# Three column blocks of the first modulation moved from TensorE to VectorE at the start of a two-layer diffusion backbone

## Chip, cores and metric

The kernel runs on one core of a Trainium2 chip. The metric is the device time of one execution in microseconds (us); lower is better. TensorE is written PE in the rows of the profile, VectorE DVE, ScalarE ACT, GpSimd POOL, and SP is the engine that issues most of the transfers.

## The reference, cut to what matters

Each of two layers modulates its input with a shift and a scale that come from the conditioning, projects it, mixes tokens in four branches, and goes on to an MLP. Only the very beginning of layer 0 bears on the change:

```
def _layer(x, cond, lp, mixer_fn):
    mod = jax.nn.silu(cond) @ lp['w_ada'] + lp['b_ada']
    sh1, sc1, g1, sh2, sc2, g2 = jnp.split(mod[:, None, :], 6, axis=-1)
    y, extra = mixer_fn(x * (1 + sc1) + sh1)
    ...
def _project(h, lp):
    ...
    (q_lat, kv_lat, k_pe, ...) = jnp.split(h @ lp['w_in'], split_at, axis=-1)
```

There are 384 tokens (128 with the conditioning `c_ctx`, 256 with `c`), D_MODEL is 1024, and everything is float32. The transposed input `h` is 8 blocks of 128 channels. Each block needs 128 shifts and 128 scales for two conditionings: one *unit* of `mod`, a product of silu(cond) with a 1024 x 256 piece of `w_ada`.

## The kernel before

A product in near float32 precision is made of three matmuls: an operand is split into a high part (fp32r) and a low remainder, `x = xh + xl`, and xh·wh, xh·wl and xl·wh are added up in PSUM. ScalarE makes the high part of a weight tile (a CAST, line 281), VectorE the low one (`split_low`, line 125).

The start of layer 0 (lines 470 to 557) interleaves three things for k = 0 to 7:

- `first_part(k)`: the modulation product of unit k on TensorE (line 330: eight small f32 matmuls of 32 x 256, sixteen records), whose bank ScalarE copies to `adap` (line 333).
- `first_input(k)`: `ada_finish` turns `adap` round with two TensorE transposes (line 339); VectorE sums the four row groups (341), adds the bias into `modT` (343) and 1 to the scale (492). Then ScalarE writes the high part of the modulated input, `hTh` (496, two instructions), VectorE the full value `hx` (497) and the low part `hTl` (125).
- `chunk(banks, w, n, k)`: nine matmuls of block k with the weights of branch A (`banks_a`, 416 columns, tiles named `o`) or of branch C (`banks_c`, 512 columns, tiles `wh` and `wl`). First the high parts (lines 520, 521), then the three that read `hTl` (518). `within` is called after the second of the three token blocks, so `ada_finish` of a coming unit stands inside a chunk.

I call the A chunk of block k a(k) and the C chunk c(k). `split_w(i)` splits the weights for blocks 2i and 2i+1. The loop runs over pairs: a(k), product k+1, c(k), the split, product k+2, a(k+1), c(k+1); the last two chunks are c(7), a(7). TensorE's order is pinned to the program by `in_order`; the other engines' instructions are placed by the scheduler. The DMA queue of SP loads everything in the order of use: two 512 KB pieces of `w_ada` per unit, the input block, and two weight tiles per pair.

After the map ScalarE evacuates the banks (`evac_to`, line 594, tiles `tmc`, `tma`); the next projection (lines 120 to 122) needs one of the C banks back. `cond_rows` (lines 226 to 233) makes `csr`, the silu of both conditionings on all 128 partitions, from a broadcast load of 1 MB: four tanh on ScalarE and eight instructions on VectorE, behind the map. `csr` feeds `ada_vector` (line 370), which computes later modulation columns on VectorE as sums of products along rows: one custom instruction of 128 x 1024 for each 128 columns and conditioning.

## Time and profile before

| | |
|---|---|
| median of 3 runs | 1311.73 us (1308.55 to 1313.06) |
| profiled execution, its own time | 1311.86 us |
| span of its instructions | 1310.1 us, so 1.8 us lie around it |
| mean granted TensorE clock | 0.993 |
| start of the first chunk, a(0) | 10.30 us |
| start of the first matmul behind the map | 56.25 us |

The profiled execution lies 0.13 us above the median. TensorE is the engine that is busy for nearly all of the span. [...]

### The profile page before, as it was taken

What the parts mean: (1) busy time and instruction counts of PE and PEld (TensorE: products, weight loads), DVE (VectorE), ACT (ScalarE), POOL (GpSimd) and SP (SyncE); (2) the same over time, 40 slices, a digit from 0 to 9 for tenths busy, and PEclk for the clock granted to TensorE, in tenths of its full rate; (3) what the DMA queues carried; (4) which work ended last, traced back from release to release, by engine and by line L of the source; (5) the groups of instructions that cost most, each with busy time, mean ns of one, the idle gap of its engine ahead of it and who ended that gap; (6) DMA issues with size and microseconds to landing.
All of it is one profiled execution on the core that took longest, in us unless ns stands there. A gap on an engine that the chain in (4) does not pass through costs nothing. (4 is left out here: it accounts for less than half of the span.)

```text
span 1310.1 us, 19402 instructions
## 1 busy us (share of the span) xinstructions
PE 1273.6 (97%) x7350; PEld 1143.7 (87%) x7350; DVE 882.9 (67%) x1603; ACT 572.7 (44%) x1054; POOL 207.2 (16%) x218
## 2 busy tenths in 40 slices
PE   8899999999999999999999999999999899999996
PEld 5789888999987999999988988899998799999995
DVE  4555899996669999543484689967455893333336
ACT  4454345323534444454365545423343644444441
POOL 0010301323223000000071120012320600000003
PEclk9999999999999999999999999999999999999998
DMA  9832354666534888554313224553644263335321
GB/s 368 295 109 91 103 173 158 210 217 222 163 112 163 274 272 271 177 171 140 113 72 121 86 93 161 182 173 118 227 159 153 72 225 129 129 129 183 133 71 49
DMA packets 64686, 211.68 MB, mean 162 GB/s; under 512 B 9233, under 2 KB 13265, under 8 KB 64465
## 3 DMA queue, kind: packets, MB, share of 16 engines
q1 hardware_dynamic: 61872, 201.49, 45.6%
q0 software_dynamic: 2432, 8.42, 1.9%
q8 instruction: 58, 0.95, 0.3%
q10 hardware_dynamic: 288, 0.52, 0.1%
q14 instruction: 36, 0.29, 0.1%
HBM read 206.28 MB, written 4.13 MB: 161 GB/s over the span
## 5 line engine op out<-in xcount | busy, mean ns | idle before, releaser
L125 DVE TENSOR_TENSOR wl<-raw,wh 128x1024 fp32r<-128x1024 f32 x250 | 317.5, 1274 | 284.9 <-ACT wh L281 281.2
L281 ACT CAST wh<-raw 128x1024 fp32r<-128x1024 f32 x250 | 261.7, 1050 | 453.3 <-PE bank L121 300.0
L120 PE MATMUL bank<-hTh,wh 128*128 128x384 f32 x976 | 330.8, 339 | 0.0
L122 PE MATMUL bank<-hTh,wl 128*128 128x384 f32 x976 | 328.1, 336 | 0.0
L121 PE MATMUL bank<-hTl,wh 128*128 128x384 f32 x976 | 328.0, 336 | 0.0
L120 PEld LDWEIGHTS bank<-hTh,wh 128*128 128x128 f32 x976 | 183.8, 188 | 6.7 <-issue 2.2
L121 PEld LDWEIGHTS bank<-hTl,wh 128*128 128x128 f32 x976 | 183.7, 188 | 2.4 <-issue 0.3
L122 PEld LDWEIGHTS bank<-hTh,wl 128*128 128x128 f32 x976 | 183.7, 188 | 0.6 <-issue 0.3
L121 PE MATMUL bank<-wl,uh 128*128 128x512 f32 x384 | 150.4, 392 | 0.0
L122 PE MATMUL bank<-wh,ul 128*128 128x512 f32 x384 | 150.2, 392 | 0.0
L120 PE MATMUL bank<-wh,uh 128*128 128x512 f32 x384 | 149.4, 391 | 0.0
L370 DVE CUSTOM_DVE_ANT_0 acc<-raw,csr,bT 128x1024 bf16<-128x1024 f32 x80 | 103.7, 1319 | 0.0
L120 PE MATMUL bank<-wh,hTh 128*128 128x256 f32 x336 | 100.6, 299 | 2.8 <-ACT tmc L594 2.8
L1107 POOL TENSOR_TENSOR tt<-tt,tt 128x384 f32<-128x384 f32 x48 | 61.6, 1304 | 242.3 <-DVE tt L1106 235.7
L370 DVE CUSTOM_DVE_ANT_0 acc<-lnc,csr,bT 128x1024 bf16<-128x1024 f32 x80 | 99.6, 1278 | 0.0
L121 PE MATMUL bank<-wl,hTh 128*128 128x256 f32 x336 | 96.0, 286 | 0.0
L122 PE MATMUL bank<-wh,hTl 128*128 128x256 f32 x336 | 95.9, 285 | 0.0
L120 PEld LDWEIGHTS bank<-wh,uh 128*128 128x128 f32 x384 | 72.0, 188 | 15.4 <-ACT wh L281 0.8
L122 PEld LDWEIGHTS bank<-wh,ul 128*128 128x128 f32 x384 | 72.0, 188 | 15.0
L121 PEld LDWEIGHTS bank<-wl,uh 128*128 128x128 f32 x384 | 72.1, 188 | 13.8
L120 PEld LDWEIGHTS bank<-wh,hTh 128*128 128x128 f32 x336 | 64.7, 193 | 6.8 <-ACT tmc L594 3.1
L121 PEld LDWEIGHTS bank<-wl,hTh 128*128 128x128 f32 x336 | 64.8, 193 | 2.5 <-issue 1.6
(260 smaller groups left out, 1862.3 us busy)
## 6 DMA issues: line engine op xcount, KB each, us to landing
raw<-in_w_g_dram SPq DMA_DIRECT2D x64, 512.0 KB, 3.6
raw<-in_w_d_dram SPq DMA_DIRECT2D x64, 512.0 KB, 3.5
raw<-in_w_u_dram SPq DMA_DIRECT2D x58, 512.0 KB, 3.7
raw<-in_w_av_dram SPq DMA_DIRECT2D x40, 512.0 KB, 3.4
lnc<-in_w_av_dram SPq DMA_DIRECT2D x40, 512.0 KB, 4.4
raw<-in_w_q_dram SPq DMA_DIRECT2D x28, 512.0 KB, 4.5
raw<-in_w_ada_dram SPq DMA_DIRECT2D x16, 512.0 KB, 8.5
raw<-in_w_b_dram SPq DMA_DIRECT2D x16, 512.0 KB, 3.6
```

Source lines behind the costliest of these rows:

```text
L120: mm(out, lhsT=a_hl[0], rhs=b_hl[0], start=start, stop=False)
L121: mm(out, lhsT=a_hl[0], rhs=b_hl[1], start=False, stop=False)
L122: mm(out, lhsT=a_hl[1], rhs=b_hl[0], start=False, stop=stop)
L125: nc.vector.tensor_tensor(out=low, in0=x, in1=high.bitcast(F32), op=ALU.subtract)
L281: nc.scalar.copy(wh, raw)
L370: nc.vector.tensor_tensor_reduce(out=alloc().bitcast(BF16), in0=w, in1=csr[:, c], scale=1.0, scalar=bT[:, l, u, b:b + 1], op0=ALU.mult, op ...
L1107: nc.gpsimd.tensor_tensor(out=acc[c], in0=acc[c], in1=t_, op=ALU.add)
```

## The change

Units 3, 5 and 7 are no longer multiplied on TensorE. Their pieces of `w_ada` are stored transposed (`w_as`), and VectorE sums them along rows against `csr` (`row_sums`, four custom instructions for each unit), bias included, straight into `modT`. For that `csr` must exist early: `cond_rows` now loads 8 KB into one partition, TensorE spreads it over 128 partitions by four f32 matmuls with a row of halves, and ScalarE and VectorE make x·(1 + tanh x) of the banks. In the units that stay on TensorE, a product with a 0/1 matrix `sel` takes the place of the transposes and of VectorE's sum. The 1 for the scale is added to the bias once. Except for unit 0, `hx` is now written by ScalarE. The first weights are loaded in two pieces and split in four; three more warm-up matmuls stand ahead of a(0). The first two stream tiles are split by name ahead of c(7), as the scheduler did before. `in_order()` now pins ScalarE and VectorE to the program's order as well.

```
-    def cond_rows(alloc):
-        nc.sync.dma_start(out=csr, in_=a["cond"].partition_broadcast(P))
...
+    def cond_rows(banks, alloc):
+        crow, half = alloc([1, 2 * D], "crow", 1), alloc([1, P], "half", 1)
+        nc.scalar.dma_start(out=crow, in_=a["cond"].rearrange("(o c) d -> o (c d)", o=1))
+        nc.vector.memset(half, 0.5)
...
+            mm(b, lhsT=half, rhs=crow[:, i:i + 512], start=True, stop=True)
+        for c, h, b in parts:
+            th = alloc([P, 512], "th", 2)
+            nc.scalar.activation(th, b, AF.Tanh)
+            nc.vector.scalar_tensor_tensor(out=csr[:, c, h * 512:(h + 1) * 512], in0=th, scalar=1.0, in1=b, op0=ALU.add,
+                                           op1=ALU.mult)
...
         for b in range(2):
-            nc.tensor.transpose(pt[:, b * P:(b + 1) * P], part[:, b * P:(b + 1) * P], ident)
-        red = sb.tile([P, 2, 2], F32, tag="adar", name=nm("adar"), bufs=2)
...
+            mm(pt[:, 2 * b:2 * b + 2], lhsT=part[:, b * P:(b + 1) * P], rhs=sel, start=True, stop=True)
...
+                def row_sums(k, c):
+                    if k in ROW_UNITS:
+                        for b in range(2):
+                            junk = st.tile([P, 512], F32, tag="junk", name=nm("junk"), bufs=1)
+                            nc.vector.tensor_tensor_reduce(
+                                out=junk.bitcast(BF16), in0=inputs[k][0][b], in1=csr[:, c], scale=1.0,
+                                scalar=bT[:, 0, k, b:b + 1], op0=ALU.mult, op1=ALU.add,
+                                accum_out=modT[0][:, k, b, c:c + 1])
...
+                        else:
+                            nc.scalar.activation(hx[:, cs], xk[:, cs], AF.Identity, bias=sh, scale=m)
                     split_low(hT[1][:, k, :], hx, hT[0][:, k, :])
...
-                with in_order((mybir.EngineType.PE,)):
+                with in_order():
...
                     for k in range(0, KT, 2):
...
                             split_w(k // 2 + 1)
                             first_part(k + 2)
                             chunk(banks_a, w_a, A_W, k + 1, lambda: first_input(k + 2))
+                            for c in range(2):
+                                row_sums(k + 3, c)
                             chunk(banks_c, w_c, 512, k + 1)
                         else:
+                            for i in range(SPLITS_AHEAD):
+                                stream.split(i)
```

**ScalarE, from the input of block 1 to that of block 3.** `adap` is the copy of a unit's product, `o` and `wh` are the weights' high parts, `hTh` and `hx` the modulated input. Before:

```order
L333 COPY adap_299<-bank_290 128x256
L281 CAST o_282<-raw_141 128x832
L496 ACTIVATE hTh<-xk_139,modT_102,ms_114 128x256
L496 ACTIVATE hTh<-xk_139,modT_102,ms_114 128x128
L281 CAST wh_286<-raw_143 128x1024
L333 COPY adap_350<-bank_341 128x256
```

Now (`adap_325` and `xk_140` belong to unit 2, `xk_150` to unit 3):

```order
L529 ACTIVATE hx_297<-xk_134,modT_102 128x128
L529 ACTIVATE hx_297<-xk_134,modT_102 128x256
L289 CAST o_308<-raw_142 128x832
L289 CAST wh_312<-raw_144 128x1024
L340 COPY adap_325<-bank_316 128x256
L521 ACTIVATE hTh<-xk_140,modT_102 128x128
L521 ACTIVATE hTh<-xk_140,modT_102 128x256
L529 ACTIVATE hx_335<-xk_140,modT_102 128x128
L529 ACTIVATE hx_335<-xk_140,modT_102 128x256
L521 ACTIVATE hTh<-xk_150,modT_102 128x128
L521 ACTIVATE hTh<-xk_150,modT_102 128x256
```

The copy of a unit's product stood ahead of the two CASTs and now stands behind both; two `hx` follow each pair of `hTh`.

**VectorE, the same stretch.** `wl` and the second `o` are the low parts of the weights; an ISA row with `junk` is one row sum. Before:

```order
L343 TENSOR_TENSOR modT_102<-adar_308,bT 128x4
L492 TENSOR_SCALAR ms_114<-modT_102 128x2
L497 TENSOR_SCALAR hx_312<-xk_139,ms_114,modT_102 128x256
L497 TENSOR_SCALAR hx_312<-xk_139,ms_114,modT_102 128x128
L125 TENSOR_TENSOR o_283<-raw_141,o_282 128x832
L125 TENSOR_TENSOR hTl<-hx_312,hTh 128x384
L125 TENSOR_TENSOR wl_287<-raw_143,wh_286 128x1024
```

Now, from `modT` of unit 2 to `modT` of unit 4:

```order
L348 TENSOR_TENSOR modT_102<-bank_331,bT 128x4
L127 TENSOR_TENSOR hTl<-hx_335,hTh 128x384
L506 ISA junk_346,modT_102<-raw_146,csr,bT 128x1024
...
L506 ISA junk_352,modT_102<-raw_148,csr,bT 128x1024
L506 ISA modT_102 128x1
L127 TENSOR_TENSOR hTl<-hx_376,hTh 128x384
L127 TENSOR_TENSOR o_388<-raw_158,o_387 128x832
L127 TENSOR_TENSOR wl_392<-raw_160,wh_391 128x1024
L348 TENSOR_TENSOR modT_102<-bank_410,bT 128x4
```

The four row sums of unit 3 stand behind `hTl` of unit 2, and `hTl` of unit 3, two weight splits and `modT` of unit 4 stand behind them.

**ScalarE, the end of the map.** `acc` is the tanh of `csr`, `tmc` a copy of a C bank. Before:

```order
L281 CAST wh_635<-raw_191 128x1024
L281 CAST wh_641<-raw_193 128x1024
L231 ACTIVATE acc_587<-csr 128x512
L231 ACTIVATE acc_591<-csr 128x512
L231 ACTIVATE acc_595<-csr 128x512
L231 ACTIVATE acc_599<-csr 128x512
L594 COPY tmc_613<-bank_238 128x512
```

Now:

```order
L529 ACTIVATE hx_534<-xk_182,modT_102 128x256
L289 CAST wh_545<-raw_188 128x1024
L289 CAST wh_549<-raw_190 128x1024
L289 CAST wh_605<-raw_192 128x1024
L289 CAST wh_611<-raw_194 128x1024
L650 COPY tmc_591<-bank_267 128x512
```

The four tanh are gone from this place; behind `tmc` all engines keep their order of before.

## Rows read from the trace of the kernel before

**Rows 1.** The page's part 1: busy time of each engine, share, instructions.

```profile
PE 1273.6 (97%) x7350; PEld 1143.7 (87%) x7350; DVE 882.9 (67%) x1603; ACT 572.7 (44%) x1054; POOL 207.2 (16%) x218
```

**Rows 2.** Windows: stretch and its length, busy time of each engine, granted clock.

```profile
core 0: us, PE busy (x) PEld busy (x) DVE busy (x) ACT busy (x) POOL busy (x), PEclk, DMA share, GB/s
8.20:11.60 3.40, 1.08 (x4) 0.82 (x5) 2.73 (x8) 2.76 (x5) 0.00 (x0) 1.00 1.03 410
...
20.00:50.00 30.00, 29.47 (x197) 22.20 (x197) 16.34 (x42) 12.93 (x24) 0.00 (x0) 1.00 1.02 382
52.60:56.00 3.40, 0.88 (x5) 0.52 (x3) 3.37 (x6) 3.02 (x6) 0.00 (x0) 1.00 0.83 286
56.00:59.40 3.40, 3.15 (x14) 3.15 (x15) 3.36 (x7) 2.40 (x6) 0.94 (x2) 0.50 0.24 69
60.00:1310.00 1250.00, 1221.59 (x7037) 1105.43 (x7035) 850.64 (x1527) 544.43 (x1004) 205.67 (x210) 1.00 0.46 153
312.00:315.40 3.40, 1.46 (x10) 1.17 (x9) 2.46 (x7) 1.30 (x2) 3.13 (x5) 1.00 0.61 206
```

**Rows 3.** Timeline, first 16 us: start, duration, instructions, idle before and releaser.

```profile
1.20 3.76 PE L541 MATMUL bank<-zero 128*128 128x256 f32 x8 [1.20 <-DVE zero L474]
...
9.92 0.33 SPq L272 DMA_DIRECT2D raw<-in_w_c_dram  x1
...
10.30 0.45 PE L520 MATMUL bank<-o,hTh 128*128 128x416 f32 x1 [2.11 <-ACT o L506]
...
15.24 0.50 PE L520 MATMUL bank<-wh,hTh 128*128 128x512 f32 x1
```

**Rows 4.** Timeline, 20 to 47 us, two rounds of the loop.

```profile
20.24 0.16 DVE L343 TENSOR_TENSOR modT<-adar,bT 128x4 f32<-128x4 f32 x1
20.64 0.99 ACT L496 ACTIVATE hTh<-xk,modT,ms 128x256 fp32r<-128x256 f32 x2 [0.52 <-DVE ms L492]
21.23 1.02 DVE L125 TENSOR_TENSOR o<-raw,o 128x832 fp32r<-128x832 f32 x1
21.54 1.04 ACT L281 CAST wh<-raw 128x1024 fp32r<-128x1024 f32 x1
22.17 0.55 DVE L125 TENSOR_TENSOR hTl<-hx,hTh 128x384 fp32r<-128x384 f32 x1
...
24.64 1.07 PE L330 MATMUL bank<-raw,cs 128*32 128x256 f32 x16
...
25.64 0.50 PE L520 MATMUL bank<-wh,hTh 128*128 128x512 f32 x1
...
40.97 0.16 DVE L343 TENSOR_TENSOR modT<-adar,bT 128x4 f32<-128x4 f32 x1
...
46.34 0.50 PE L520 MATMUL bank<-wh,hTh 128*128 128x512 f32 x1
```

**Rows 5.** Groups by line and shape, first 54 us: busy, mean ns, idle before.

```profile
L333 ACT COPY adap<-bank 128x256 f32<-128x256 f32 x8 | 3.0, 373 | 20.2 <-PE bank L330 20.2
...
L281 ACT CAST o<-raw 128x832 fp32r<-128x832 f32 x3 | 2.7, 889 | 0.0
```

**Rows 6.** Timeline, the end of the map.

```profile
49.28 3.88 ACT L281 CAST wh<-raw 128x1024 fp32r<-128x1024 f32 x4
...
53.54 2.19 ACT L231 ACTIVATE acc<-csr 128x512 f32<-128x512 f32 x4 [0.38 <-DMA csr<-in_cond_dram]
...
55.64 1.54 ACT L594 COPY tmc<-bank 128x512 f32<-128x512 f32 x3
...
56.25 0.58 PE L120 MATMUL bank<-wh,hTh 128*128 128x256 f32 x1 [2.77 <-ACT tmc L594]
```

**Rows 7.** Timeline of VectorE, one row sum between others, later in the kernel.

```profile
419.34 1.28 DVE L370 CUSTOM_DVE_ANT_0 acc<-lnc,csr,bT 128x1024 bf16<-128x1024 f32 x1
420.55 0.08 DVE L370 DVE_READ_ACCUMULATOR2_ANT modT<- 128x1 f32 x1
```

**Rows 8.** DMA issues of the first 60 us: size, median us to landing.

```profile
raw<-in_w_c_dram SPq DMA_DIRECT2D x4, 512.0 KB, 8.5
```

## The prediction

> **What bounds the kernel now.** I read the page's engine table first: TensorE is busy 1273.6 us of a span of 1310.1 [rows 1]. Then the windows. From 60 us on TensorE is busy 1221.6 of 1250 us [rows 2], and the order of every engine behind the map is unchanged. So a shift at the point where the next stage starts (56.25, [rows 6]) goes to the end one for one; nothing later takes it up. The question is when TensorE starts that stage, and at which clock it runs until then.

> Three stretches matter, and the timeline of each says what ended last.

> *The start.* a(0) begins at 10.30, c(0) at 15.24 [rows 3]. At 11.6 the clock fell to 0.50 behind 3.4 us in which TensorE was busy for 1.08 [rows 2]; that is why the nine matmuls of a(0) and one product lie 4.94 us ahead of c(0).

> *The rounds.* c(2) begins at 25.64, c(6) at 46.34 [rows 4]: a round of two blocks takes (46.34 − 25.64)/2 = 10.35 us. In 20 to 50 us TensorE is busy 29.47 of 30 and the transfers hold all queues (share 1.02, 382 GB/s) [rows 2]. TensorE alone sets the round; VectorE (16.34) and ScalarE (12.93) have a third and more to spare.

> *The end of the map.* Four CASTs run from 49.28 to 53.16; then ScalarE waits 0.38 us for the 1 MB load of `csr`, does four tanh (53.54 to 55.73), and only then copies `tmc`, for which TensorE waited 2.77 us [rows 6]. Busy for 0.88 of 3.4 us, TensorE falls to half clock again and does 3.15 us of work at 0.50 [rows 2]. At full clock that work takes half: 1.58 us are lost.

> **The change, step by step.**

> *TensorE's work.* Units 3, 5 and 7 take three products of 1.07 us off it [rows 4], with the gap behind each 1.2, and the transposes with them, about 0.2: 1.4 us each, 4.2 in all. This shows in the time only if TensorE stays what the round waits for.

> *The start.* Four f32 matmuls of 512 columns now stand ahead of the first product. The nearest row is the warm-ups: 1024 columns in 3.76 us at half clock [rows 3]; 2048 at full clock take as long, less some 0.25 for the first one's start, so 3.5. From 4.96 that is 8.45; product 1.07, `adap` 0.37 [rows 5], `sel` and `modT` 0.4 and 0.16, `hTh` 0.99 [rows 4]: a(0) at about 11.5 in place of 10.30. `sel` has no row; two matmuls of two columns lie between a bare 0.2 and 0.6, and I take 0.4, the transposes' own size. If the clock were still half in part of the four matmuls, up to 1.7 more. The gap ahead of a(0) is now filled with matmuls, so I take the full clock through a(0): 1.7 for it and 1.2 for the product, c(0) at 14.4, 0.8 earlier than before.

> *The rounds.* Here ScalarE and VectorE now follow the program, and the sums stand between the two inputs of a round. I follow one round from `modT` of unit 2 to `modT` of unit 4 through the two orders shown with the change:

> - `modT` and the hand-over, 0.16 + 0.04 [rows 4].
> - `hTh` of unit 2, 0.90 (20.64 to the next operation at 21.54, [rows 4]) and two `hx` of the same shapes, now on ScalarE, 0.98: 1.88, hand-over 0.04.
> - `hTl`, 0.55 in its row [rows 4], of which some 0.47 before the next starts.
> - four row sums. A later one takes 1.21 to its read and 0.08 for that [rows 7]; back to back 4 × 1.21 + 0.08 = 4.92. They read another tile in their second operand's place and the same shape, so I bound one by 1.15 and 1.35.
> - `modT` of unit 3 is complete only now: `hTh` and `hx` of unit 3, 1.92 with the hand-over.
> - CAST `o` stands behind them on ScalarE: 0.89 [rows 5], 0.84 with the hand-over and less its tail; `hTl` of unit 3 lies beside it.
> - the split of `o`, 1.02 [rows 4], 0.95 to the next one; the CAST of `wh`, 1.04 [rows 4], beside it; the split of `wl`, 1.14.

> Sum: 0.20 + 1.88 + 0.04 + 0.47 + 4.92 + 1.92 + 0.84 + 0.95 + 1.14 = 12.36 us, then `modT` of unit 4. Its `adap` and `sel` are earlier, behind the CAST of `wh`. TensorE needs only 10.35 − 1.4 = 8.95 for the same round. So the chain through the two small engines is the longer by 3.4, and longer than the old round by 2.0: that is what I expect to bind. Queued behind the sums are `hTl` of unit 3, both splits and the next `modT`; TensorE waits for them at `sel` of units 4 and 6 and ahead of a(3) and a(5).

> [...] In the trace `hTl` starts at 22.17, 0.54 after its `hTh` was there (20.64 + 0.99), because the split of `o` stood ahead of it [rows 4]. [...]

> *Where the chain starts.* `modT` of unit 1 at 16.05 (c(0) at 14.4, four matmuls, `sel`), its input to 17.95, two CASTs to 19.7, the split of `wl` to 20.9, `modT` of unit 2 at 21.05; it was 20.24 + 0.16 = 20.40 [rows 4], so 0.65 late. The weights for it are there: the tile issued at 9.92 [rows 3] lands 8.5 later [rows 8], at 18.4. Two rounds on, `modT` of unit 6 ends at 21.05 + 24.7 = 45.75, where it was 41.13 [rows 4].

> *The end.* From 45.75: `hTh` and `hx` of unit 6, 1.92; `hTl` 0.47; four sums 4.92; `hTh` and `hx` of unit 7, 1.92: ScalarE is free at 55.0. Four CASTs of 0.95 (3.88 for four, [rows 6]), to 58.75; `tmc` 0.5: TensorE starts the next stage at 59.3 in place of 56.25, **3.05 us later**. The tanh, 2.57 us with their wait, are gone from here, but what the sums add ahead is more. c(7) starts when `hTh` of unit 7 is there (54.0), a(7) ends near 58, so the wait for `tmc` shrinks from 2.77 to some 1.2 and the half clock behind it has no cause: −1.58. The same walk through the kernel before puts its last CAST's end 0.4 early; I add that.

> Sum: +3.05 − 1.58 + 0.4 = **+1.9 us**. Against the profiled execution (span 1310.1, 1311.86 with what lies around it, 0.13 above the median of the three runs) that gives 1313.8.

> **The rivals.** About 0.3%, 3.9 us, is what a measurement of this kernel can tell from no change: 1307.8 to 1315.7.

> *TensorE sets the round after all, faster.* For it: TensorE is the bound of 20 to 50 us now [rows 2]. Then the start gives 0.8, three units 1.4 each, the end its wait of 2.77, the half clock 1.58: 0.8 + 4.2 + 2.8 + 1.6 = 9.4 less, 1302.5. It decides if a chain round is below 8.95, that is if 3.4 us of it lie side by side: two sums in each round would have to cost nothing. The order speaks against it.

> *The round stays at 10.35, faster by a little.* The transfers were at 1.02 of their queues in 20 to 50 us [rows 2] and the bytes are the same, so they may set the pace; a chain 2 us shorter than I add up would do the same. Then only the end's wait and half clock go: −4.3, 1307.5.

> *The clock falls in the new waits, slower.* In a round of 12.4 us TensorE has 8.95 of work; it waits some 2.4 ahead of what follows `sel` and some 1.7 ahead of c(7). All falls in the trace stand behind stretches with TensorE busy for 0.88 to 1.46 of 3.4 us [rows 2], as before 315.4. A fall inside a round is paid by the chain's slack; one that lasts into the end stage costs up to 1.6 as at 56.0, and one ahead of c(7) delays c(7), a(7) and `tmc` by 1.0 to 1.7. With sums of 1.35 (twelve, +1.7) the next stage starts at 61.0. Together +1.9 + 1.6 + 1.7 = 1317; the fall alone gives 1315.4, and it passes the bound when the sums are above 1.23 or the four cond matmuls run at half clock. [...]

> **How the numbers follow.** The chain binds as added up and the clock holds, or one fall of about 1 us: 1313.8, chance 0.55, own range 1311.5 to 1315.7. Slower rival 0.23 (1315.5 to 1319). Round unchanged 0.14 (1306 to 1309.5, half of it beyond the bound). TensorE-bound 0.08 (1302.5). Faster: 0.08 + some 0.09 = 0.17; slower 0.23 + 0.02 = 0.25; same 0.58. The range leaves out the TensorE-bound case, the lower half of the unchanged round and the far end of the slower rival: 1308 to 1318.

> **What the changed kernel's profile would show.** Right: a(0) near 11.5 and c(0) near 14.4 at clock 1.00; `modT` of unit 2 near 21.0 and of unit 6 near 45.7; between them VectorE and ScalarE each waiting for the other, never both for a transfer; TensorE idle some 2 us a round behind `adap` and CAST; the next stage at 59.3 behind `tmc`, with no half clock behind it. Wrong: TensorE busy all through 20 to 50 us and c(6) ahead of 45; a row sum far from 1.21; VectorE waiting for a piece of `w_ada`; the clock at 0.50 anywhere between 40 and 62 us. What would make the number wrong most easily is the chain: each 0.1 us in its round comes three times, and each in `sel` or the cond matmuls once.

## The result, and the profile after

| | before | changed |
|---|---|---|
| median | 1312.39 us (8 runs) | 1321.97 us (8 runs, 1315.33 to 1323.84) |
| profiled execution: its time, span | 1311.86, 1310.1 | 1323.44, 1321.7 |
| a(0), c(0) | 10.30, 15.24 | 17.70, 21.62 |
| `modT` of unit 2, of unit 6 (end) | 20.40, 41.13 | 28.31, 52.82 |
| first matmul of the next stage | 56.25 | 66.33 |

The changed kernel is slower: ratio 1.0067, interval 1.0051 to 1.0084, or +8.8 us on 1312.39. The forecast was +1.9, and the range ended at 1318.

Most of it is lost before 22 us. The timeline of the changed kernel, its start (start, duration, instructions, idle before and releaser):

```profile
1.20 3.78 PE L585 MATMUL bank<-zero 128*128 128x256 f32 x8 [1.20 <-DVE zero L478]
...
4.91 7.19 PE L236 MATMUL bank<-crow,half 1*128 1x512 f32 x8
...
12.03 1.94 PE L337 MATMUL bank<-raw,cs 128*32 128x256 f32 x16
...
14.48 1.01 PE L347 MATMUL bank<-sel,adap 128*128 128x2 f32 x4 [0.52 <-ACT adap L340]
15.36 2.91 PE L585 MATMUL bank<-zero 128*128 128x256 f32 x6
...
17.70 0.91 PE L562 MATMUL bank<-o,hTh 128*128 128x416 f32 x1
...
19.10 0.55 PE L563 MATMUL bank<-o,hTh 128*128 128x416 f32 x1
...
19.78 0.35 PE L563 MATMUL bank<-o,hTh 128*128 128x416 f32 x1
...
21.62 0.50 PE L562 MATMUL bank<-wh,hTh 128*128 128x512 f32 x1
```

The four cond matmuls take 7.19 us, the product 1.94 where it was 1.07 [rows 4], and the matmuls of a(0) 0.55 each until 19.10 and 0.35 from 19.78: by these durations all of this start runs at half clock. The granted clock that the profile gives can't be read here. It says 1.00 for the whole start (4.91 to 12.03 and 12.03 to 19.74), and this trace holds no change of clock ahead of 19.74; the durations of equal matmuls tell the clock.

The rounds, same view. Two of the `modT` rows (40.41 and 52.67) come 12.25 and 12.26 us behind the one before; between the first two stand the row sums (`junk`), the inputs of unit 3 and the CASTs:

```profile
28.16 0.15 DVE L348 TENSOR_TENSOR modT<-bank,bT 128x4 f32<-128x4 f32 x1
...
30.73 1.28 DVE L506 CUSTOM_DVE_ANT_0 junk<-raw,csr,bT 128x1024 bf16<-128x1024 f32 x1
...
33.38 0.50 ACT L521 ACTIVATE hTh<-xk,modT 128x128 fp32r<-128x128 f32 x1 [3.16 <-DVE modT L506]
...
36.04 0.60 ACT L521 ACTIVATE hTh<-xk,modT 128x256 fp32r<-128x256 f32 x1 [2.16 <-DVE modT L506]
36.54 0.97 ACT L529 ACTIVATE hx<-xk,modT 128x128 f32<-128x128 f32 x2
...
37.42 0.87 ACT L289 CAST o<-raw 128x832 fp32r<-128x832 f32 x1
...
38.20 1.04 ACT L289 CAST wh<-raw 128x1024 fp32r<-128x1024 f32 x1
...
39.14 0.36 ACT L340 COPY adap<-bank 128x256 f32<-128x256 f32 x1
39.27 1.23 DVE L127 TENSOR_TENSOR wl<-raw,wh 128x1024 fp32r<-128x1024 f32 x1
39.56 0.61 PE L347 MATMUL bank<-sel,adap 128*128 128x2 f32 x4 [2.22 <-ACT adap L340]
...
40.41 0.15 DVE L348 TENSOR_TENSOR modT<-bank,bT 128x4 f32<-128x4 f32 x1
...
52.67 0.15 DVE L348 TENSOR_TENSOR modT<-bank,bT 128x4 f32<-128x4 f32 x1
...
66.33 0.39 PE L122 MATMUL bank<-wh,hTh 128*128 128x256 f32 x1 [1.02 <-ACT tmc L650]
```

And the windows (stretch, length, busy time of each engine, granted clock, share of the transfer queues, GB/s):

```profile
40.22:43.63 3.41, 3.41 (x10) 2.94 (x10) 1.48 (x4) 1.86 (x4) 0.00 (x0) 0.50 0.86 239
66.33:69.74 3.41, 3.40 (x28) 3.41 (x29) 2.63 (x8) 2.36 (x6) 0.46 (x2) 1.00 0.16 42
681.93:685.34 3.41, 3.34 (x11) 3.24 (x12) 2.13 (x6) 1.33 (x3) 3.33 (x3) 0.50 0.38 154
1043.74:1047.15 3.41, 2.99 (x11) 2.99 (x12) 2.13 (x6) 1.26 (x3) 3.25 (x4) 0.50 0.00 0
```

The next stage now starts at clock 1.00, where it was 0.50 [rows 2]. Two later stretches, at 681.93 and 1043.74, ran at half clock here and not in the profile before; they hold 3.34 and 2.99 us of TensorE's work, so by my estimate they cost half of it, 1.67 + 1.50 = 3.2. The spans then close: 66.33 − 56.25 = 10.1 later at the next stage, −1.6 for its clock, +3.2 for the two stretches, 11.7 of a difference of 11.6. The two stretches lie in a part that the change leaves alone, and the runs below have both (e10), one (e9) or neither (e2, e3), so I count them to this execution and not to the change: 10.1 − 1.6 = 8.5, beside 8.8 by the ratio of the runs.

### The profile page after: what moved, and what is told of

It reads as the page before. It is cut to its first block, busy times and chain, and to the rows that moved or that the text cites. A ratio compares the mean times of both kernels' runs of the same rounds, so it can differ in the third digit from the quotient of the medians.

```text
span 1321.7 us, 19332 instructions
## 1 busy us (share of the span) xinstructions
PE 1283.9 (97%) x7320; PEld 1150.7 (87%) x7320; DVE 889.8 (67%) x1594; ACT 578.0 (44%) x1066; POOL 205.6 (16%) x218
## 5 line engine op out<-in xcount | busy, mean ns | idle before, releaser
L127 DVE TENSOR_TENSOR wl<-raw,wh 128x1024 fp32r<-128x1024 f32 (+1 forms) x251 | 315.9, 1262 | 285.5 <-ACT wh L289 278.7
L376 DVE CUSTOM_DVE_ANT_0 acc<-raw,csr,bT 128x1024 bf16<-128x1024 f32 x80 | 103.7, 1320 | 0.0
L123 PEld LDWEIGHTS bank<-wl,uh 128*128 128x128 f32 x384 | 72.1, 188 | 13.8
```

The costliest lines, as they stand in the source:

```text
L123: mm(out, lhsT=a_hl[0], rhs=b_hl[1], start=False, stop=False)
L127: nc.vector.tensor_tensor(out=low, in0=x, in1=high.bitcast(F32), op=ALU.subtract)
L376: nc.vector.tensor_tensor_reduce(out=alloc().bitcast(BF16), in0=w, in1=csr[:, c], scale=1.0, scalar=bT[:, l, u, b:b + 1], op0=ALU.mult, op ...
```

## The experiments

The question was which part costs the 7 us beyond the forecast. Theory A: the one-row cond matmuls neither bring nor hold the full clock, and the start pays for it. Theory B: when the clock rises is chance. Theory C: the row sums, or the rounds, cost it. All ratios are to the kernel before, run beside on the same chip. Each run was profiled once, so its places in time are those of one execution.

**e1: cond matmuls of 128 rows.**

```
-        crow, half = alloc([1, 2 * D], "crow", 1), alloc([1, P], "half", 1)
-        nc.scalar.dma_start(out=crow, in_=a["cond"]...)
+        crow, half = alloc([P, 2 * D], "crow", 1), alloc([P, P], "half", 1)
+        nc.vector.memset(crow[:, 0:D], 0.0)
+        nc.gpsimd.memset(crow[:, D:], 0.0)
+        nc.scalar.dma_start(out=crow[0:1], in_=a["cond"]...)
```

> The four cond matmuls get operands of 128 rows (row 0 holds the data, the other rows zeros) in place of one row; columns and count are the same. Theory A (matmuls of one row do not bring TensorE to full clock, so the whole start runs at half clock): the clock is 1.00 long before 12 us, the four take 3.5 to 4.5 us in place of 7.19, a(0) starts near 12 in place of 17.70, the next stage near 60 in place of 66.3, and the time is about 6 us below the changed kernel, near 1315. Theory B (when the clock rises is chance and the rows have no part in it): a(0) near 17.7 as often as before, time as the changed kernel, near 1321. Theory C (the row sums in the rounds cost the time): also near 1321, with rounds of 12.25.

Ratio 1.0031 (1.0014 to 1.0049), median 1316.66. The timeline of e1:

```profile
6.62 3.67 PE L238 MATMUL bank<-crow,half 128*128 128x512 f32 x8 [1.81 <-DMA crow<-in_cond_dram]
...
13.50 0.54 PE L564 MATMUL bank<-o,hTh 128*128 128x416 f32 x1
13.88 0.35 PE L565 MATMUL bank<-o,hTh 128*128 128x416 f32 x1
```

3.67 us in place of 7.19 for the same columns. a(0) comes at 13.50 and not near 12, since the zeros stand ahead of the load of `crow`, for which TensorE waits 1.81. The next stage starts at 61.17, 5.2 sooner than in the changed kernel, and the interval of the ratio lies below the changed kernel's: B and C alone would have left the time where it was. But in this execution the clock had risen at 4.53, ahead of these matmuls, and e3 below shows such a rise (at 4.46) with one-row matmuls behind it. So not all of the 5.2 is due to the rows.

**e2: eight warm-ups of 128 rows ahead of the one-row matmuls.**

```
-WARM = (4, 3)
+WARM = (8, 3)
```

> Eight warm-up matmuls of 128 rows in place of four ahead of the one-row cond matmuls. They end near 7 with the clock risen. Theory A: one-row matmuls do not hold the clock either; it falls to 0.50 within or right behind them, a(0) near 16 or later, time near 1320. Theory B: the clock stays at 1.00, the four take 3.6, a(0) near 13.8, time about 4 below the changed kernel, near 1317.

Ratio 1.0046 (1.0028 to 1.0064), median 1318.3. Timeline and windows of e2:

```profile
6.96 3.70 PE L236 MATMUL bank<-crow,half 1*128 1x512 f32 x8
...
12.98 2.91 PE L585 MATMUL bank<-zero 128*128 128x256 f32 x6
15.33 0.91 PE L562 MATMUL bank<-o,hTh 128*128 128x416 f32 x1
```

```profile
8.90:12.33 3.43, 2.85 (x22) 0.99 (x21) 2.75 (x6) 2.38 (x5) 0.00 (x0) 1.00 1.02 414
12.33:15.74 3.41, 3.41 (x11) 2.88 (x12) 2.44 (x7) 2.61 (x6) 0.00 (x0) 0.50 1.04 409
```

With the clock up before them the one-row matmuls take 3.70, beside 3.67 for those of 128 rows in e1: in these two executions one row in place of 128 cost 0.03 us by itself. But behind them the clock falls at 12.33, with TensorE busy 2.85 of 3.43, and a(0) runs at half clock (0.50 from 12.33 on; its matmuls take 0.55). A expected a(0) at 16 or later and a time near 1320; B, with the clock held, a(0) at 13.8 and 1317. a(0) came at 15.33, and the time between the two: the fall speaks for A, but TensorE also waited 0.57 us in the stretch ahead of it, so that e2 alone doesn't decide.

**e3: units 3, 5 and 7 back on TensorE, all else as changed.**

```
+SUMS = ()
...
-                    if k not in ROW_UNITS:
+                    if k not in SUMS:
```

> Units 3, 5 and 7 go back to TensorE; no row sums, all else as changed, csr included. Theory A: a(0) still at 17.7 and c(0) at 21.6; the rounds go back to some 10.4 from 12.25, TensorE-bound; next stage near 61 in place of 66.3, time near 1316: still 4 above the kernel before. Theory C (the sums are the whole loss): time at or below the kernel before, 1312 or less.

Ratio 1.0032 (1.0017 to 1.0048), median 1316.74: C is wrong as the whole, since 4.2 us of the loss stay without any sum. Windows and timeline of e3:

```profile
4.46:7.87 3.41, 3.41 (x10) 1.41 (x8) 1.21 (x2) 1.48 (x3) 0.00 (x0) 1.00 1.05 378
7.87:11.28 3.41, 2.89 (x19) 0.68 (x17) 1.70 (x5) 1.42 (x4) 0.00 (x0) 0.50 0.99 378
```

```profile
4.71 4.11 PE L237 MATMUL bank<-crow,half 1*128 1x512 f32 x8
...
14.42 0.91 PE L563 MATMUL bank<-o,hTh 128*128 128x416 f32 x1
...
35.35 1.04 ACT L290 CAST wh<-raw 128x1024 fp32r<-128x1024 f32 x1
...
36.30 0.36 ACT L341 COPY adap<-bank 128x256 f32<-128x256 f32 x1
...
36.71 0.61 PE L348 MATMUL bank<-sel,adap 128*128 128x2 f32 x4 [0.92 <-ACT adap L341]
```

In this execution the clock rose at 4.46, near the first recorded change of the kernel before (4.79), and fell at 7.87 behind a stretch in which TensorE was busy for all of 3.41 us, nearly all of it with one-row matmuls. That is the plainest sight of A. It also shows that B has a part: up to a(0) this program is that of the changed kernel, and yet the clock rose at 4.46 and not at 19.74, and a(0) came at 14.42 and c(0) at 19.04, where I expected 17.7 and 21.6. Of the 3.4 us by which the next stage (62.97) comes sooner than in the changed kernel, 2.6 are there at c(0) already, and 0.8 are gained behind it, where the sums are gone. My number for the rounds was wrong, too: c(2) to c(4) and c(4) to c(6) take 12.0 each, not 10.4. The copy `adap` stands behind both CASTs and TensorE waits for it; a(3) to c(3) takes 3.46 where it took 2.04. So without any sum a wait of 0.92 for this copy gives nearly the changed round. That the pin alone does it isn't shown: e10 below has no pin on ScalarE and no sums, and two of its rounds also take 12.0.

**e4: only TensorE pinned.**

```
-                with in_order():
+                with in_order((mybir.EngineType.PE,)):
```

> Only TensorE is pinned to the program in the start stage; the scheduler then puts the copy of a product ahead of the two CASTs and modT of units 2, 4 and 6 ahead of the two weight splits. If the chain through ScalarE and VectorE is what a round of 12.25 waits for, taking the two splits (0.95 + 1.14) out from ahead of modT gives rounds near 10.2, the next stage near 62 in place of 66.3, time near 1317. If the sums or the transfers alone set the round, it stays at 12.25 and the time near 1321. The start (a(0) near 17.7) does not change.

Ratio 1.0026 (1.0010 to 1.0043), median 1317.94. a(0) at 17.69 as in the changed kernel, rounds of 10.88, 10.77 and 10.76, next stage at 64.25 (expected 62). The same view of e4:

```profile
38.34 0.87 ACT L289 CAST o<-raw 128x832 fp32r<-128x832 f32 x1
38.46 0.56 DVE L127 TENSOR_TENSOR hTl<-hx,hTh 128x384 fp32r<-128x384 f32 x1 [1.16 <-ACT hx L529]
38.48 0.50 PE L347 MATMUL bank<-sel,adap 128*128 128x2 f32 x4
...
39.02 0.16 DVE L348 TENSOR_TENSOR modT<-bank,bT 128x4 f32<-128x4 f32 x1
...
39.24 1.02 DVE L127 TENSOR_TENSOR o<-raw,o 128x832 fp32r<-128x832 f32 x1
```

`modT` now stands ahead of the split, `sel` waits for nothing, and a round is 1.5 shorter with all sums in it. The chain through ScalarE and VectorE was real. What a round waits for now is `hTh` of unit 3, behind the sums: 1.35 us in a(3).

**e5: the kernel before with csr loaded and its tanh done inside the loop.**

```
+                    if k == 3:
+                        nc.sync.dma_start(out=csr, in_=a["cond"].partition_broadcast(P))
...
+                        if k in (2, 4):
+                            cond_row(k // 4, 0, st.tile([P, 512], ...))
...
-            cond_rows(lambda: t2("acc"))
```

> The kernel before, with one part alone: the 1 MB load of csr goes between the inputs of blocks 3 and 4 and the four tanh with their VectorE work are placed inside the loop, so nothing but the CASTs stands ahead of tmc. If the end of the map is worth what the prediction took (a wait of 2.77 and 1.58 at half clock): next stage near 54 in place of 56.25, wait ahead of it under 0.7, time 2 to 4 below the kernel before. If the load or the tanh are paid in the rounds: c(6) later than 46.34 by what was gained.

Ratio 0.9999 (0.9986 to 1.0011). The wait at the end went as said, but the next stage starts at 58.94 and not near 54: the rounds paid for it (c(6) at 51.58 in place of 46.34, though 0.85 of that is there at c(0) already). Timeline of e5:

```profile
32.66 0.63 ACT L228 ACTIVATE th<-csr 128x512 f32<-128x512 f32 x1 [0.43 <-DVE csr L230]
...
33.19 0.35 ACT L330 COPY adap<-bank 128x256 f32<-128x256 f32 x1
...
33.60 0.45 PE L336 MATMUL bank<-ident,adap 128*128 128x128 f32 x2 [2.27 <-ACT adap L330]
...
58.94 0.38 PE L120 MATMUL bank<-wh,hTh 128*128 128x256 f32 x1 [0.22 <-ACT tmc L596]
```

The wait for `tmc` is 0.22 in place of 2.77. But the scheduler put all four tanh in a row, each behind VectorE's work on one before, and the `adap` of unit 4 behind them: TensorE waits 2.27 and then runs at half clock (0.55 for a matmul of an A chunk that took 0.35 ahead of the wait). In the medians gain and loss cancel.

**e6: e1 and e4 together.**

```
+        crow, half = alloc([P, 2 * D], "crow", 1), alloc([P, P], "half", 1)
...
+                with in_order((mybir.EngineType.PE,)):
```

> The two mends together: cond matmuls of 128 rows, and only TensorE pinned. If the two causes are separate, their gains add: next stage at 66.3 - 5.2 - 2.1 = 59.0, rounds of 10.8, a(0) near 13.5, time about that of the kernel before, within 2 us. If they overlap (the later start gave the transfers time that is now missing), next stage at 60 or later.

Ratio 0.9998 (0.9987 to 1.0008), next stage at 58.93. The two mends bring the change back to the time of before, so these two account for the loss in the time; the interval lies below that of e4, from which only the rows differ. The place 58.93 is in part luck, for the way to it was another than expected: a(0) came at 15.25 in place of 13.5, and the rounds took 10.0, 9.8 and 10.8 in place of 10.8 each. The cond matmuls of e6:

```profile
6.69 5.22 PE L238 MATMUL bank<-crow,half 128*128 128x512 f32 x8 [1.72 <-DMA crow<-in_cond_dram]
```

This row tells A from B better than e1. 5.22 us lie between the 3.67 of full clock (e1) and the 7.19 of half clock (changed kernel): by that the clock was still at half here when the 128-row matmuls began, and it rose while they ran (first change in this trace at 9.81). In the changed kernel and in e4 it did not rise during 7.19 us of one-row matmuls without a gap (first changes at 19.74 and 20.49).

**e7 and e8: csr by the broadcast load, no cond matmuls** (e7 without sums, e8 with them and with the load behind block 1; only TensorE pinned).

```
-                    cond_rows([bank(psa), bank(psa), bank(psa), bank(pso)], ...)
+                    if k == 3:
+                        nc.sync.dma_start(out=csr, in_=a["cond"].partition_broadcast(P))
+                nc.gpsimd.tensor_scalar(out=th, in0=th, scalar1=0.5, scalar2=0.5, op0=ALU.mult, op1=ALU.add)
```

> No matmuls for csr at all: csr comes by the broadcast load between blocks 3 and 4 with its tanh inside the loop; units 3, 5 and 7 on TensorE, only TensorE pinned; sel, first weights in pieces, three warm-ups ahead of a(0) stay. If the one-row matmuls were what held the clock and the start: a(0) near 9.8 at clock 1.00, c(0) near 13, rounds near 10.5, next stage near 52, time 4 to 6 below the kernel before. If the start is late for another reason of the change, a(0) stays above 13.

> As e7, but with the row sums on VectorE as changed; the broadcast load stands ahead of block 2, its tanh ahead of the first round. Rounds of 10.8 as in e4, since the sums stay; a(0) near 9.8; next stage near 56, time 1 to 3 below the kernel before and above e7: the sums then cost what lies between the two. If taking work off TensorE pays once the start is mended, it comes out below e7.

e7: 1.0020 (1.0008 to 1.0033), e8: 1.0006 (0.9993 to 1.0018). e7's a(0) comes at 9.88 and c(0) at 13.39, as theory A has it without cond matmuls. e8's does not:

```profile
12.17 0.91 PE L555 MATMUL bank<-o,hTh 128*128 128x416 f32 x1
```

On TensorE the program of e8 up to here is that of e7, but the first change of clock in its trace is at 13.81: the start ran at half clock into a(0) (its first matmul took 0.91, as in the changed kernel) without any one-row matmul. The start can thus be late by chance, too, as B has it; the latest first changes, 19.74 and 20.49, are those of the changed kernel and of e4, with one-row matmuls. The rest missed: next stage at 61.97 and 63.02. As in e5 four tanh in a row stand ahead of an `adap`; `sel` waits for it 2.82 in e7 and 2.83 in e8. Neither says what the sums cost.

**e9 to e11: the four cond matmuls behind the first product** (`rows` gives one at each step, one ahead of `sel` and three behind it; 128 rows, only TensorE pinned; e9 with all sums, e10 with none, e11 with those of units 3 and 5).

```
                     first_part(0)
+                    next(rows)
                     first_input(0, split_first)
-                    warm_up(WARM[1])
+                    for _ in rows:
+                        pass
```

> On top of e6 (128 rows, only TensorE pinned) the four cond matmuls go behind the first product, one ahead of sel and three ahead of a(0), in place of the three warm-ups. They then lie in time in which TensorE waits for the copy, modT and hTh anyway: a(0) near 11.6 in place of 13.5, c(0) near 14.5, next stage near 57, time 1 to 3 below the kernel before. If the start is bound by ScalarE (copy, tanh, hTh, CASTs in one row), a(0) stays above 13 and the time equals e6.

> As e9, units 3, 5 and 7 on TensorE. Without the sums, rounds are TensorE's own, 10.4 to 10.6; hTh of unit 7 doesn't wait for sums at the end, so the map ends sooner: next stage near 54, time 3 to 5 below the kernel before and 1 to 3 below e9. If the sums take work off a binding TensorE, e9 is the faster of the two.

> As e9, with sums for units 3 and 5 only; unit 7 on TensorE. The sums of unit 7 stand alone ahead of c(7) (nothing on TensorE to lie beside them): without them the end is shorter by some 3, while the rounds stay at 10.8. Next stage near 54.5, time 2 to 4 below the kernel before. If the end is bound by the four CASTs instead, as e9.

e9: 0.9989 (0.9977 to 1.0001); e10: 1.0001 (0.9989 to 1.0014); e11: 0.9987 (0.9975 to 1.0000). e9's a(0) comes at 10.89, c(0) at 14.09, the next stage at 56.37: the start is mended. e10 missed: its next stage is at 57.14, and its rounds are 12.0, 12.0 and 10.8. The scheduler puts both weight splits ahead of `hTl` of unit 2, and TensorE waits 0.89 for it in the first round; but e9 has the same wait (0.89) and rounds of 10.9, 10.8 and 10.8. What e10's first two rounds have beyond it is a third product on TensorE. So in these executions the sums shorten the first two rounds by 1.1 and 1.2 us, and the end gives most of it back: from c(6) to the next stage 9.88 in e9 and 7.95 in e10. e11 missed as well: next stage at 57.13 (expected 54.5), since its last round, with the product of unit 7 and half clock from 42.39 to 45.80, takes 13.4; its end is shorter than e9's by 1.9 (expected 3). The sums and their absence come out the same within the intervals; e9 and e11 have the lower ratios, but that the sums pay isn't shown.

**e12: the kernel before with nothing but csr changed**, by four cond matmuls of 128 rows behind the first product (the edits of e1 and e9 made in the kernel before).

```
-            cond_rows(lambda: t2("acc"))
...
+                    rows = cond_rows((psa, pso, psg, psg), ...)
                     first_part(0)
+                    next(rows)
                     first_input(0)
+                    for _ in rows:
+                        pass
```

> The kernel before, with one part of the change alone and in its mended form: csr by four cond matmuls of 128 rows, one behind the first product and three ahead of a(0), in place of the 1 MB load and the tanh at the end of the map. hx stays on VectorE, all units on TensorE, no sel. Rounds of 10.35 as before, no wait for the tanh: a(0) near 11, c(0) near 14.3, next stage near 53 with a wait under 1 ahead of it and no half clock behind, time 3 to 5 below the kernel before and below e9. If the cond matmuls cost what the end gains, within 1 of the kernel before.

Ratio **0.9969 (0.9957 to 0.9981)**, median 1308.87 beside 1313.64: faster than the kernel before and than the changed one. Below e9 it isn't shown, since the intervals overlap. Timeline and windows of e12:

```profile
51.07 3.92 ACT L289 CAST wh<-raw 128x1024 fp32r<-128x1024 f32 x4
...
54.90 1.54 ACT L605 COPY tmc<-bank 128x512 f32<-128x512 f32 x3
55.52 0.38 PE L120 MATMUL bank<-wh,hTh 128*128 128x256 f32 x1 [0.26 <-ACT tmc L605]
```

```profile
20.00:50.00 30.00, 30.00 (x210) 22.82 (x203) 15.53 (x40) 12.44 (x23) 0.00 (x0) 1.00 0.97 371
55.52:58.90 3.38, 3.38 (x28) 3.38 (x29) 2.65 (x10) 2.35 (x6) 0.40 (x2) 1.00 0.21 27
```

`tmc` follows the CASTs at once, TensorE waits 0.26, and the stage behind runs at clock 1.00. In this execution a(0) came late (13.49, half clock from 7.44 to 10.86), so 55.52 is not as early as the 53 that I expected; c(2) to c(6) are rounds of 10.35 as before. In this execution 0.7 us of the gain are seen in the place of the next stage and 1.6 in its clock; where the rest comes from isn't traced.

## Why the prediction was wrong, by its own steps

**The start: this step failed.** "2048 at full clock take as long, less some 0.25 …, so 3.5" and "I take the full clock through a(0)". Both clocks were wrong. What was forecast beside what the trace has: cond matmuls to their end 8.45, now 12.0; product 1.07, now 1.94; `sel` 0.4, now 1.01; three warm-ups that I took as free cover 2.91 and held a(0) to 17.70, though its `hTh` and weights were there by 16.7; a(0) itself 2.9 to c(0)'s product in place of 1.7. c(0) comes at 21.62 in place of 14.4: **7.2 us**, and 1.9 + 7.2 = 9.1 is what was measured (8.8). How much of the 7.2 is chance isn't known: e3, with the same start but the clock up from 4.46 to 7.87, reached c(0) at 19.04, 4.6 late. The bound that I wrote for it, "up to 1.7 more", was too narrow: I let the clock be half for part of four matmuls, not for all that followed them up to a(0). A one-row f32 matmul stood in no row of the profile; I had taken its effect on the clock from the warm-ups, whose rows are full. The runs show the difference: a first change of clock at 9.81 in e6 beside 20.49 in e4, and in e3 a fall at 7.87.

**The rounds: right in size.** Forecast 12.36 from `modT` to `modT`; measured 12.25 and 12.26. From `modT` of unit 2 on the forecast runs 7.26 early, at unit 6 7.07, at the next stage 7.0: the mistake of the start, carried unchanged. That the sum is so near is in part luck. The row sums follow one another every 1.33, so the four take 5.31 (30.73 to 36.04) where I had 4.92; and `hTh` and `hx` of unit 3 take only 1.38 behind them (36.04 to 37.42) where I had 1.92, since the first `hTh` starts behind two sums already (33.38). The two errors cancel. And the step named too few causes: the sums are one way to a round of 12, the CASTs ahead of `adap` another (12.0 in e3 without sums). The rival "TensorE sets the round after all" had its condition wrong for the same reason: taking every sum away did not bring it, neither in e3 nor in the first two rounds of e10.

**The end: right.** From `modT` of unit 6 to the next stage it takes 13.51 (forecast 13.55). The wait for `tmc` is 1.02 (forecast 1.2), with no half clock behind it. I priced that part of the change at 4.3, without what it costs to make csr early; e12 gains 4.1 in all (0.0031 × 1312), with what its start costs.

**The clock rival: the right kind, in the wrong place.** I looked for a fall in the waits of the rounds. There is one (40.22, behind TensorE's wait of 2.22), and the chain absorbs it, as written: the next `modT` still comes 12.26 later. What counted was the clock that did not rise (no recorded change ahead of 19.74). The four falls in the changed kernel's trace ahead of its last microseconds stand behind 1.19, 1.43, 1.72 and 1.66 us of TensorE's work in some 3.4, beside 0.88 to 1.46 in the prediction; the falls of e2 and e3 stand behind more. A wait could bear on e2, where TensorE was busy 2.85 of 3.43 us and waited 0.57 ahead of `sel`, but not on e3, where it was busy for all of the 3.41 us ahead of the fall. That ScalarE and VectorE keep to the pinned order was an assumption of the chain. In e3 the copy `adap` starts at 36.30, behind the CASTs of 34.57 and 35.35 that it doesn't need and 1.47 us after its product ended (34.83), and lifting the pin in e4 takes 1.5 us off a round (10.8 in place of 12.25); both agree with the assumption.

**The chances.** Slower by over 0.3% had 0.25, and the slower rival's sum ended at 1319. The median of the runs is 1322, outside the range.

Open: why the clock rises at 4.46 in one execution (e3) and only at 9.81 (e6), 13.81 (e8) or 19.74 in others that start with the same four warm-ups. The spread of the changed kernel, 1315.33 to 1323.84, may in part be this chance: its two shortest runs (1315.33 and 1317.99) are the two with a mean granted clock of 0.990, the other six have 0.992 to 0.994. Since the half clock of its start isn't recorded as such (1.00 up to 19.74), more recorded half clock in less time fits a start like e3's. That is argued, since one execution alone was profiled; and a start like e3's gives 2.6 us at c(0), not the 6.6 between the shortest run and the median.

## What to carry to other kernels

Price an operation that TensorE has not run before twice: its time at either granted clock (here 3.70 and 7.19 us for the one-row matmuls), and what clock follows it until the next rise. Here the two parts were alike: of the 7.2 us by which c(0) came late, about 3.6 were there at the end of the cond matmuls (12.0 in place of 8.45) and as much came behind them. With one row padded to 128 with zeros a(0) came at 13.50 in e1 (17.70 in the changed kernel) and at 15.25 in e6 (17.69 in e4). A pinned order has to be read for what each instruction must wait behind: in e3 TensorE waited 0.92 us for one small copy behind two casts, in rounds of 12.0 without any sum, beside 12.25 with four sums in the chain. A single profile of a start whose clock varies from run to run (first change at 4.46 in e3, at 19.74 in the changed kernel) is one draw: put the ratios of many runs beside it. And when a change mixes a gain with a loss, make its parts alone: the part that pays (e12) needed neither the sums nor the new order.
